# The eleven expert blocks computed during the one-hot stage: from one fp32 matmul on the raw weights to three matmuls on a rounded part and a rest, both made on GpSimd

## The chip, the cores and the metric

The kernel runs on one core of a Trainium2 chip. The metric is the device time of one execution in microseconds (us), the median of the runs shown. The engines are named as in the profile: PE is TensorE (with PEld, its weight loads), DVE is VectorE, ACT is ScalarE, POOL is GpSimd, SP is the engine that issues the DMAs here.

## The reference, cut to what matters

The program is a network of two blocks of two layers each for 256 tokens of width 1024. The second block ends each layer with a sparse feed-forward of 16384 experts (128 blocks of 128). For each token and each of 8 heads it picks 16 experts, and adds up their outputs:

```python
xt = hn.reshape(T, D_MODEL)
# idx, gate: the 16 chosen experts of each token and head, and their softmax weights
ub = u_tab[ib]
vb = v_tab[ib]
act = jax.nn.gelu(jnp.einsum('td,thkd->thk', xb, ub).astype(F32), approximate=False)
return jnp.einsum('thk,thkd->td', (gb * act).astype(vb.dtype), vb)
```

The kernel doesn't gather. It computes the activation of all 16384 experts for all tokens, multiplies it with a matrix of gates that is zero for experts not chosen, and multiplies the result with all of `peer_v`.

## The kernel before, in words

All of this is in `peer(l)`, which runs twice, once for each layer of the second block. Its parts, in the order of the program:

1. The normalised input is transposed into `xT`, a pair of tiles: `xTh`, rounded to the type fp32r, and `xTl`, the rest. An addition on DVE (L1640) puts the two together again as `xT32`, in full fp32.
2. `route` finds the chosen experts, above all on DVE. Meanwhile the activations of expert blocks 0 to 35 (`NB` = 36) are computed by `act`: a block's weights (128 x 1024, 512 KB) come by DMA into `raw`, ACT casts them into `hi` (fp32r), GpSimd subtracts to get `lo` (L290, `eng` is `nc.gpsimd`), and `mm3` issues three fp32r matmuls for each of 8 slices: hi with xTh, hi with xTl, lo with xTh.
3. **The one-hot stage** builds the gate matrix `G` (experts by tokens) four tokens at a time, in 64 steps. `one_hot` makes two tiles of comparisons on DVE, `B` (L1677) and `A` (L1679); the gates are multiplied into `A` on ACT (L1681), and for one token of every second step on DVE (L1683). Four fp32 matmuls multiply A and B into the PSUM bank `gps` (L1703). DVE multiplies the first 36 blocks of the result into `G` (L1705), and ACT copies the other 92 (L1706). `one_hot` runs three steps ahead of the matmuls.
4. In every sixth step of that stage (tokens 8, 32, 56, ... 248, eleven times) one expert block from 36 on is computed ahead. Its `raw` weights go straight into eight fp32 matmuls with `xT32` (L1696, on the trace two PE instructions each), into half a PSUM bank that is kept until the stage is over.
5. Then the rest: activations of blocks 47 to 127, and the product with `peer_v` into `pacc`.

Tiles come from pools of rotating buffers: a tile waits until the tile that had its buffer has been read for the last time. `raw`, `hi` and `lo` have three buffers each, and the tiles of `one_hot` (`oh`) are taken from the same buffers, in turns under the tags `hi` and `lo`. `gps` has two PSUM banks. A scheduler sets the order in which instructions stand on each engine when the program is built; on the chip each engine works through its queue in that order.

Of the kernel before, what the change touches and what calls it, by code (L numbers as in the profile page):

```python
# [10 lines left out]
F32 = mybir.dt.float32  # L11
# [5 lines left out]
OP = mybir.AluOpType  # L17
# [3 lines left out]
S, D, P = 256, 1024, 128  # L21
# [176 lines left out]
class Net:  # L198
# [90 lines left out]
        self.nc.scalar.copy(out=hi, in_=src)  # L289
        (eng or self.nc.vector).tensor_tensor(out=lo, in0=src, in1=hi.bitcast(F32), op=OP.subtract)  # L290

    def chunk(self, ap, n, raw_only=False, eng=None):

        raw = self.wp.tile([P, 1024], F32, tag="raw", name="raw", bufs=3)
        self.nc.sync.dma_start(out=raw[:, :n], in_=ap)
        if raw_only:
            return raw[:, :n]
        hi = self.wp.tile([P, 1024], F32R, tag="hi", name="hi")
        lo = self.wp.tile([P, 1024], F32R, tag="lo", name="lo")
        self.split(raw[:, :n], hi[:, :n], lo[:, :n], eng)  # L300
        return hi[:, :n], lo[:, :n]

    def mm3(self, ps, lh, ll, rh, rl, start, stop):
# [1318 lines left out]
    def peer(self, l):  # L1622
        nc, a, c = self.nc, self.a, self.c
        with ExitStack() as st:
            xp = st.enter_context(self.tc.tile_pool(name=f"pp{l}", bufs=1))
            xT = self.norm_t(xp, f"norm_ffn_2_{l}", "xT", 3)
# [9 lines left out]
            i2T = xp.tile([P, S], F32, name="i2T")  # L1636
            gT = xp.tile([P, S], F32, name="gT")
            keep = [[xp.tile([P, P], F32, name=f"{n}{t}") for n in ("ix1", "ix2", "gt")] for t in range(2)]
            xT32 = st.enter_context(self.tc.tile_pool(name=f"px{l}", bufs=1)).tile([P, 8, S], F32, name="xT32")
            nc.vector.tensor_tensor(out=xT32, in0=xT[0].bitcast(F32), in1=xT[1].bitcast(F32), op=OP.add)  # L1640
            NB = self.NB

            def carve(lo, n):
# [7 lines left out]
            self.lin_b(xT, a[f"pwq_{l}"], lambda b, ps: nc.scalar.copy(out=qT[:, b], in_=ps))  # L1651
            turns = [self.route(l, t, qT, sub, carve, base + 24, keep[t], i1T, i2T, gT) for t in range(2)]

            def act(b, ps, eng=None):
                hi, lo = self.chunk(a[f"pu_{l}"][b].rearrange("p k n -> p (k n)"), 1024, eng=eng)
                for k in range(8):
                    sl = slice(k * P, k * P + P)
                    self.mm3(ps, hi[:, sl], lo[:, sl], xT[0][:, k], xT[1][:, k], k == 0, k == 7)
                return ps

            for b in range(NB):
                if b == 24:
                    turns[0]()
                nc.scalar.activation(out=G[:, b], in_=act(b, self.bank("ps")[:, :S], nc.gpsimd), func=AF.Gelu)
# [4 lines left out]
            ahead = []  # L1669
            def one_hot(t0):  # L1670

                oh = self.wp.tile([P, 1024], F32, tag=("hi", "lo")[t0 // TB % 2], name="oh")
                oh = oh.rearrange("p (s t a) -> p s t a", s=2, t=TB)
                A, B = oh[:, 0], oh[:, 1]
                io = lambda n: c["iota"][:, None, :].to_broadcast([P, n, P])
                tb = lambda x, n: x[:, t0:t0 + n, None].to_broadcast([P, n, P])
                nc.vector.tensor_tensor(out=B, in0=io(TB), in1=tb(i2T, TB), op=OP.is_equal)  # L1677
                na = TB - (t0 // TB) % 2
                nc.vector.tensor_tensor(out=A[:, 0:na], in0=io(na), in1=tb(i1T, na), op=OP.is_equal)  # L1679
                for t in range(na):  # L1680
                    nc.scalar.activation(out=A[:, t], in_=A[:, t], func=AF.Copy, scale=gT[:, t0 + t:t0 + t + 1])  # L1681
                for t in range(na, TB):
                    nc.vector.tensor_scalar(A[:, t], c["iota"], i1T[:, t0 + t:t0 + t + 1], gT[:, t0 + t:t0 + t + 1],  # L1683
                                            op0=OP.is_equal, op1=OP.mult)
                return A, B

            ready = [one_hot(t0) for t0 in range(0, 3 * TB, TB)]
            for t0 in range(0, S, TB):
                if t0 % 24 == 8 and len(ahead) < 11:
                    i = len(ahead) % 2  # L1690
                    if i == 0:
                        pa = self.bank("ps" if len(ahead) < 8 else "pox")
                    pi = pa[:, i * S:i * S + S]
                    w = self.chunk(a[f"pu_{l}"][NB + len(ahead)].rearrange("p k n -> p (k n)"), 1024, raw_only=True)
                    for k in range(8):
                        nc.tensor.matmul(pi, lhsT=w[:, k * P:k * P + P], rhs=xT32[:, k], start=k == 0, stop=k == 7)  # L1696
                    ahead.append(pi)
                if t0 + 3 * TB < S:
                    ready.append(one_hot(t0 + 3 * TB))
                A, B = ready.pop(0)  # L1700
                ps = self.bank("gps")
                for t in range(TB):
                    nc.tensor.matmul(ps[:, t * P:t * P + P], lhsT=A[:, t], rhs=B[:, t], start=True, stop=True)  # L1703
                pv = ps.rearrange("p (t b) -> p b t", t=TB)
                nc.vector.tensor_tensor(out=G[:, 0:NB, t0:t0 + TB], in0=G[:, 0:NB, t0:t0 + TB], in1=pv[:, 0:NB], op=OP.mult)  # L1705
                nc.scalar.copy(out=G[:, NB:, t0:t0 + TB], in_=pv[:, NB:])  # L1706
# [6 lines left out]
            for j, ps in enumerate(ahead):  # L1713
                gated(NB + j, ps)
            NA = NB + len(ahead)
            gated(NA, act(NA, self.bank("aps")[:, :S]))
            acc = [[self.bank("pacc") for _ in range(2)] for _ in range(2)]
            last = []
            for b in range(NE):
                if NA <= b < NE - 1:  # L1720
                    gated(b + 1, act(b + 1, self.bank("aps")[:, :S]))
                wh = wk.tile([P, S], F32R, name="pwh")
                wl = wk.tile([P, S], F32R, name="pwl")
                self.split(G[:, b], wh, wl)
                hi, lo = self.chunk(a[f"pv_{l}"][b], 1024)
                last.append((b, wh, wl, hi, lo))

                if b < NE - 2 or b == NE - 1:
                    for t in range(2):
                        for b_, wh, wl, hi, lo in last:  # L1730
                            for n in range(2):
                                self.mm3(acc[t][n], wh[:, t * P:t * P + P], wl[:, t * P:t * P + P],
                                         hi[:, n * 512:n * 512 + 512], lo[:, n * 512:n * 512 + 512], b_ == 0, b_ == NE - 1)
                    last = []
            hr = []
            for t in range(2):
                raw = self.wp.tile([P, 1024], F32, tag="raw", name="raw", bufs=3)
# [8 lines left out]
    NB = 36  # L1746
# [102 lines left out]
```

## Time and profile before

| what | us |
|---|---|
| median of 3 runs | 3409.68 (3405.24 to 3410.45) |
| the profiled execution | 3410.51 |
| its span in the trace | 3408.7 |
| PE busy | 3280.5 (96% of the span) |
| DVE busy | 2251.4 (66%) |
| ACT busy | 1761.8 (52%) |
| POOL busy | 240.4 (7%) |

The span goes from the first to the last instruction in the trace, and 1.8 us of the execution lie outside it. A busy share is a mean over stages with different limits, and says little of one stage. "Idle before" is time for which an engine stood still ahead of an instruction, and the arrow names what ended it. A row of the windows view has the stretch, its length, the busy time and the number of instructions of PE, PEld, DVE, ACT and POOL, PE's granted clock as a share of full speed, the DMA engines' share and their GB/s. A row of a timeline has start, duration, engine, line, operation, out<-in and shapes.

### The profile page before, as it was taken

The page shows a single profiled execution, that of the slowest core. Times are in us where ns is not written, and L with a number is a line of the kernel's source. Part 1 is how long each engine was busy: PE and PEld are TensorE (multiplying, and loading weights), DVE is VectorE, ACT ScalarE, POOL GpSimd, SP SyncE. Part 2 cuts the span into 40 slices and gives each one's busy share as a digit, 9 for nine tenths or more (in the row PEclk, how much of TensorE's full clock was granted, in tenths as well). Part 3 has the DMA queues.
Part 4 walks back from the last instruction along what each step waited for, and adds up shares of the span by engine and source line. Part 5 has one row for each costly group of instructions (what it writes and reads, how often), then busy time and mean ns, then how long its engine had stood idle before and what let it go on. Part 6 is the DMA issues. An engine that isn't in the chain of part 4 may idle for free.

```text
span 3408.7 us, 53956 instructions
## 1 busy us (share of the span) xinstructions
PE 3280.5 (96%) x20870; PEld 2894.5 (85%) x20870; DVE 2251.4 (66%) x3881; ACT 1761.8 (52%) x3226; POOL 240.4 (7%) x159
## 2 busy tenths in 40 slices
PE   8999999999998999988999999999999899999999
PEld 7678998677997988888988999988888898899998
DVE  6676556666557776589965555567658996555555
ACT  4555445554445554435944444456444495444444
POOL 0000000000000000064000000000005500000000
PEclk9999999999999999999999999999999999999999
DMA  5435665444555345543255555555544315555555
GB/s 187 145 124 188 221 207 187 138 144 155 186 188 173 128 149 179 182 142 112 82 191 187 188 189 186 187 192 172 186 157 144 127 63 192 187 189 187 186 188 177
DMA packets 161105, 570.00 MB, mean 167 GB/s; under 512 B 18256, under 2 KB 23760, under 8 KB 159824
## 3 DMA queue, kind: packets, MB, share of 16 engines
q1 hardware_dynamic: 160848, 566.56, 50.1%
q8 instruction: 163, 2.67, 0.3%
q14 instruction: 94, 0.77, 0.1%
HBM read 557.05 MB, written 9.44 MB: 166 GB/s over the span
## 4 chain that ended last, share of the span: by engine, by line
PE 62%; DVE 10%; ACT 2%; DMA 1%; issue 1%; POOL 0%; DVEq 0%; POOLq 0%; ACTq 0%; SPq 0%
PE pacc L305 7%; PE pacc L307 7%; PE pacc L306 7%; PE aps L305 5%; PE aps L306 5%; PE aps L307 4%; PE ps L307 3%; PE ps L305 3%; PE ps L306 3%; PE gps L1703 3%; PE ps L1696 2%; PE fps L305 1%; PE fps L306 1%; PE fps L307 1%; DVE G L1789 1%; DVE G L1813 1%
## 5 line engine op out<-in xcount | busy, mean ns | idle before, releaser
L290 DVE TENSOR_TENSOR lo<-raw,hi 128x1024 fp32r<-128x1024 f32 (+3 forms) x906 | 1102.8, 1218 | 795.1 <-ACT hi L289 789.8
L289 ACT CAST hi<-raw 128x1024 fp32r<-128x1024 f32 (+1 forms) x978 | 1020.1, 1044 | 932.4 <-issue 199.6
L305 PE MATMUL pacc<-hi,pwh 128*128 128x512 f32 x1024 | 404.3, 395 | 0.1
L307 PE MATMUL pacc<-hi,pwl 128*128 128x512 f32 x1024 | 403.6, 394 | 0.0
L306 PE MATMUL pacc<-lo,pwh 128*128 128x512 f32 x1024 | 402.8, 393 | 0.0
L305 PE MATMUL aps<-xTh,hi 128*128 128x256 f32 x1296 | 365.1, 282 | 0.9 <-ACT G L1706 0.9
L306 PE MATMUL aps<-xTl,hi 128*128 128x256 f32 x1296 | 365.0, 282 | 0.0
L307 PE MATMUL aps<-xTh,lo 128*128 128x256 f32 x1296 | 363.7, 281 | 0.0
L305 PE MATMUL ps<-xTh,hi 128*128 128x256 f32 x960 | 276.9, 289 | 21.5 <-ACT hi L289 17.6
L307 PE MATMUL ps<-xTh,lo 128*128 128x256 f32 x960 | 276.2, 288 | 15.0 <-POOL lo L290 15.0
L289 ACT CAST pwh<-G 128x256 fp32r<-128x256 f32 x256 | 103.8, 406 | 342.2 <-DVE G L1711 213.9
L306 PE MATMUL ps<-xTl,hi 128*128 128x256 f32 x960 | 275.0, 287 | 1.2 <-DVE xTl L290 1.2
L305 PEld LDWEIGHTS aps<-xTh,hi 128*128 128x128 f32 x1296 | 243.8, 188 | 7.8 <-ACT G L1706 1.3
L306 PEld LDWEIGHTS aps<-xTl,hi 128*128 128x128 f32 x1296 | 243.7, 188 | 7.2
L307 PEld LDWEIGHTS aps<-xTh,lo 128*128 128x128 f32 x1296 | 243.7, 188 | 0.0
L307 PEld LDWEIGHTS pacc<-hi,pwl 128*128 128x128 f32 x1024 | 192.5, 188 | 45.5 <-DVE pwl L290 0.3
L305 PEld LDWEIGHTS pacc<-hi,pwh 128*128 128x128 f32 x1024 | 192.7, 188 | 38.7 <-ACT pwh L289 1.0
L306 PEld LDWEIGHTS pacc<-lo,pwh 128*128 128x128 f32 x1024 | 193.2, 189 | 37.5
L305 PEld LDWEIGHTS ps<-xTh,hi 128*128 128x128 f32 x960 | 185.5, 193 | 23.2 <-ACT hi L289 18.5
L290 POOL TENSOR_TENSOR lo<-raw,hi 128x1024 fp32r<-128x1024 f32 x72 | 192.0, 2677 | 179.8 <-ACT hi L289 179.8
L305 PE MATMUL fps<-fTh,hi 128*128 128x256 f32 x704 | 199.8, 284 | 4.5 <-ACT fTh L289 4.5
L307 PEld LDWEIGHTS ps<-xTh,lo 128*128 128x128 f32 x960 | 185.5, 193 | 16.5 <-POOL lo L290 16.5
(652 smaller groups left out, 6961.8 us busy)
## 6 DMA issues: line engine op xcount, KB each, us to landing
raw<-in_pu_dram SPq DMA_DIRECT2D x256, 512.0 KB, 3.3
raw<-in_pv_dram SPq DMA_DIRECT2D x256, 512.0 KB, 3.3
raw<-in_wbg_dram SPq DMA_DIRECT2D x48, 512.0 KB, 3.6
raw<-in_ffg_dram SPq DMA_DIRECT2D x44, 512.0 KB, 3.3
raw<-in_ffu_dram SPq DMA_DIRECT2D x44, 512.0 KB, 3.3
raw<-in_ffd_dram SPq DMA_DIRECT2D x44, 512.0 KB, 3.3
raw<-in_win_dram SPq DMA_DIRECT2D x36, 512.0 KB, 3.3
raw<-in_pwq_dram SPq DMA_DIRECT2D x32, 512.0 KB, 3.3
```

The costliest lines, as they stand in the source:

```text
L289: self.nc.scalar.copy(out=hi, in_=src)
L290: (eng or self.nc.vector).tensor_tensor(out=lo, in0=src, in1=hi.bitcast(F32), op=OP.subtract)
L305: mm(ps, lhsT=lh, rhs=rh, start=start, stop=False)
L306: mm(ps, lhsT=lh, rhs=rl, start=False, stop=False)
L307: mm(ps, lhsT=ll, rhs=rh, start=False, stop=stop)
L1696: nc.tensor.matmul(pi, lhsT=w[:, k * P:k * P + P], rhs=xT32[:, k], start=k == 0, stop=k == 7)
L1703: nc.tensor.matmul(ps[:, t * P:t * P + P], lhsT=A[:, t], rhs=B[:, t], start=True, stop=True)
L1789: nc.vector.tensor_tensor(out=cv[:, h], in0=vv[:, h, 0, :, None].to_broadcast([P, 16, 16]), in1=vv[:, h, 1, None, :].to_broadcast([P, 16, ...
L1813: nc.vector.tensor_tensor(out=eq, in0=eq, in1=iv[:, :, s, None, :].to_broadcast([P, 8, 16, 16]), op=OP.mult)
```

## The change

The eleven blocks computed ahead are treated as the others: `act` computes them, with three fp32r matmuls for each slice. Cast and subtraction both go to GpSimd, since `chunk` gets a second engine, `cast`. `xT32` and its addition go.

```diff
-    def chunk(self, ap, n, raw_only=False, eng=None):
+    def chunk(self, ap, n, raw_only=False, eng=None, cast=None):
...
-        self.split(raw[:, :n], hi[:, :n], lo[:, :n], eng)
+        if cast is None:
+            self.split(raw[:, :n], hi[:, :n], lo[:, :n], eng)
+        else:
+            cast.tensor_copy(hi[:, :n], raw[:, :n])
+            eng.tensor_tensor(out=lo[:, :n], in0=raw[:, :n], in1=hi[:, :n].bitcast(F32), op=OP.subtract)
...
-            xT32 = st.enter_context(self.tc.tile_pool(name=f"px{l}", bufs=1)).tile([P, 8, S], F32, name="xT32")
-            nc.vector.tensor_tensor(out=xT32, in0=xT[0].bitcast(F32), in1=xT[1].bitcast(F32), op=OP.add)
...
-            def act(b, ps, eng=None):
-                hi, lo = self.chunk(a[f"pu_{l}"][b].rearrange("p k n -> p (k n)"), 1024, eng=eng)
+            def act(b, ps, eng=None, cast=None):
+                hi, lo = self.chunk(a[f"pu_{l}"][b].rearrange("p k n -> p (k n)"), 1024, eng=eng, cast=cast)
...
-                    w = self.chunk(a[f"pu_{l}"][NB + len(ahead)].rearrange("p k n -> p (k n)"), 1024, raw_only=True)
-                    for k in range(8):
-                        nc.tensor.matmul(pi, lhsT=w[:, k * P:k * P + P], rhs=xT32[:, k], start=k == 0, stop=k == 7)
-                    ahead.append(pi)
+                    ahead.append(act(NB + len(ahead), pi, nc.gpsimd, nc.gpsimd))
```

The change also moves instructions. On GpSimd, at the end of the route of the second block's first layer, the subtractions for blocks 0 to 35 were followed by the next stage's work (`r` is a reciprocal root of a later norm). Before:

```order
L290 TENSOR_TENSOR lo_15766<-raw_15763,hi_15765 128x1024
L290 TENSOR_TENSOR lo_15798<-raw_15795,hi_15797 128x1024
L290 TENSOR_TENSOR lo_15830<-raw_15827,hi_15829 128x1024
L431 TENSOR_TENSOR r_22527<-v_22525,mhalf_163 128x1
L431 TENSOR_TENSOR r_22534<-v_22532,mhalf_163 128x1
```

and in the changed kernel (the line numbers are its own):

```order
L290 TENSOR_TENSOR lo_15793<-raw_15790,hi_15792 128x1024
L290 TENSOR_TENSOR lo_15825<-raw_15822,hi_15824 128x1024
L303 CAST hi_15914<-raw_15912 128x1024
L304 TENSOR_TENSOR lo_15915<-raw_15912,hi_15914 128x1024
L303 CAST hi_16028<-raw_16026 128x1024
L304 TENSOR_TENSOR lo_16029<-raw_16026,hi_16028 128x1024
```

Eleven pairs of a cast (L303) and a subtraction (L304) stand there now, for each layer.

On PE, around the fifth block computed ahead (the one of token 104), the rows of before are these; a `gps` row is the four matmuls of one step, here from token 96 on, a `ps` row is a matmul of the block:

```order
L1703 MATMUL gps_16217<-oh_16158 128x128 x4
L1703 MATMUL gps_16231<-oh_16172 128x128 x4
L1696 MATMUL ps_16294<-xT32_13854,raw_16295 128x256 x2
L1703 MATMUL gps_16245<-oh_16186 128x128 x4
L1703 MATMUL gps_16259<-oh_16210 128x128 x4
L1696 MATMUL ps_16294<-xT32_13854,raw_16295 128x256
L1703 MATMUL gps_16273<-oh_16224 128x128 x4
```

and these stand in the changed kernel at the same block:

```order
L1702 MATMUL gps_16362<-oh_16313 128x128 x4
L309 MATMUL ps_16369<-xTh_13709,hi_16372 128x256
L310 MATMUL ps_16369<-xTl_13710,hi_16372 128x256
L1702 MATMUL gps_16407<-oh_16327 128x128 x4
L311 MATMUL ps_16369<-xTh_13709,lo_16373 128x256
L309 MATMUL ps_16369<-xTh_13709,hi_16372 128x256
...
L311 MATMUL ps_16369<-xTh_13709,lo_16373 128x256
L1702 MATMUL gps_16421<-oh_16341 128x128 x4
L1702 MATMUL gps_16435<-oh_16355 128x128 x4
```

The block's matmuls were spread over six steps; now two stand behind the step of token 100 (`gps_16362`) and 22 in one piece behind that of token 104 (`gps_16407`), ahead of the steps of tokens 108 and 112.

On DVE, from the multiplication of step 104 into `G` on, the changed kernel has these rows (L1679 makes B, L1681 makes A, L1685 one token's gates, L1704 multiplies a step's result into `G`; `oh_16414` is of token 120, `oh_16442` of token 128, `oh_16428` of token 124):

```order
L1704 TENSOR_TENSOR G_13841<-G_13841,gps_16407 128x36x4
L1679 TENSOR_TENSOR oh_16414<-cst_142,i2T_13843 128x512
L1681 TENSOR_TENSOR oh_16414<-cst_142,i1T_13842 128x512
L1679 TENSOR_TENSOR oh_16442<-cst_142,i2T_13843 128x512
L1679 TENSOR_TENSOR oh_16428<-cst_142,i2T_13843 128x512
L1704 TENSOR_TENSOR G_13841<-G_13841,gps_16421 128x36x4
```

The comparison for token 128 stands in the queue ahead of the multiplication of step 108 (`gps_16421`). By the rotation of the `hi` buffers (tokens 96, 104, 112, then the block's `hi`, then 120, 128) it takes the buffer of token 112's tile, `oh_16355`, which `gps_16435` reads.

## Rows read from the trace of the kernel before

**Rows 1.** Windows, first one-hot stage: busy us by engine, PE's granted clock, DMA.

```profile
1592.44:1689.70 97.26, 95.67 (x684) 88.99 (x684) 95.11 (x221) 90.63 (x286) 0.00 (x0) 1.00 0.18 61
```

**Rows 2.** Chain in order of time, inside the first one-hot stage: start, length, what.

```profile
1604.67 0.43 PE ps L1696 x2
...
1612.01 1.78 PE gps L1703 x16
```

**Rows 3.** DVE's timeline in the first one-hot stage: start, duration, instruction.

```profile
1642.10 0.30 DVE L1705 TENSOR_TENSOR G<-G,gps 128x144 f32<-128x144 f32 x1
1642.32 0.69 DVE L1677 TENSOR_TENSOR oh<-cst,i2T 128x512 f32<-128x512 f32 x1
1642.92 0.56 DVE L1679 TENSOR_TENSOR oh<-cst,i1T 128x384 f32<-128x384 f32 x1
1643.39 0.30 DVE L1705 TENSOR_TENSOR G<-G,gps 128x144 f32<-128x144 f32 x1
1643.60 0.35 DVE L1683 TENSOR_SCALAR oh<-cst,i1T,gT 128x128 f32<-128x128 f32 x1
1643.86 0.69 DVE L1677 TENSOR_TENSOR oh<-cst,i2T 128x512 f32<-128x512 f32 x1
```

**Rows 4.** PE's timeline, matmuls in three parts.

```profile
1413.60 0.28 PE L306 MATMUL ps<-xTl,hi 128*128 128x256 f32 x1
1413.72 0.28 PE L307 MATMUL ps<-xTh,lo 128*128 128x256 f32 x1
```

**Rows 5.** DVE's timeline, the addition for `xT32` and the instruction behind it.

```profile
1414.37 2.29 DVE L1640 TENSOR_TENSOR xT<-xTh,xTl 128x2048 f32<-128x2048 f32 x1
1417.52 1.23 DVE L290 TENSOR_TENSOR lo<-raw,hi 128x1024 fp32r<-128x1024 f32 x1 [0.87 <-ACT hi L289]
```

**Rows 6.** POOL's timeline, three subtractions at the end of the first route.

```profile
1581.69 3.52 POOL L290 TENSOR_TENSOR lo<-raw,hi 128x1024 fp32r<-128x1024 f32 x1 [1.41 <-ACT hi L289]
1585.17 4.44 POOL L290 TENSOR_TENSOR lo<-raw,hi 128x1024 fp32r<-128x1024 f32 x1
1589.57 2.39 POOL L290 TENSOR_TENSOR lo<-raw,hi 128x1024 fp32r<-128x1024 f32 x1
```

**Rows 7.** DVE's timeline around the same time.

```profile
1568.17 0.22 DVE L1808 TENSOR_SCALAR G<-G 128x128 uint32<-128x128 uint32 x1
...
1577.97 2.39 DVE L1808 TENSOR_SCALAR G<-G 128x128 uint32<-128x128 uint32 x1
...
1580.66 2.29 DVE L1811 TENSOR_TENSOR G<-G,cst 128x2048 f32<-128x2048 f32 x1
1582.99 4.37 DVE L1813 TENSOR_TENSOR G<-G 128x2048 f32<-128x2048 f32 x1
1587.39 2.29 DVE L1814 TENSOR_REDUCE ix<-G 128x128 f32<-128x2048 f32 x1
1589.67 2.85 DVE L1677 TENSOR_TENSOR oh<-cst,i2T 128x512 f32<-128x512 f32 x1
```

**Rows 8.** A group of POOL by line, then one timeline row each of POOL and DVE.

```profile
L1552 POOL MEMSET hq<- 128x2048 f32 x1 | 1.8, 1812 | 67.3 <-DVE hqe L1538 67.3
...
71.53 1.22 POOL L672 COPY kcr<-rot 128x128 f32<-128x128 f32 x1 [39.70 <-DVE rot L523]
...
71.38 1.22 DVE L290 TENSOR_TENSOR lo<-raw,hi 128x1024 fp32r<-128x1024 f32 x1
```

**Rows 9.** ACT's timeline: the gates of four tokens, then a copy into G.

```profile
1607.01 1.28 ACT L1681 ACTIVATE oh<-oh,gT 128x128 f32<-128x128 f32 x4
1608.19 0.45 ACT L1706 COPY G<-gps 128x368 f32<-128x368 f32 x1
```

**Rows 10.** Windows in the first route, columns as in Rows 1.

```profile
1505.00:1510.00 5.00, 0.79 (x2) 0.50 (x2) 5.00 (x5) 4.31 (x7) 2.78 (x1) 0.65 0.00 0
1510.00:1515.00 5.00, 3.52 (x16) 3.52 (x17) 5.00 (x3) 0.00 (x0) 5.00 (x3) 0.50 0.41 117
...
1525.00:1530.00 5.00, 3.06 (x24) 2.64 (x23) 5.00 (x30) 1.33 (x2) 5.00 (x3) 1.00 0.53 161
```

## The prediction, made before the changed kernel ran

> **What bounds the kernel now.** The change touches two stretches, the one-hot stages of the two layers, so I read them before anything else. First the windows over the first stage, from DVE's second one-hot instruction to its last [rows 1]: in 97.3 us PE is busy for 95.7, DVE for 95.1, ACT for 90.6 and POOL for nothing, at full clock. The second stage reads alike. So three engines are full at once, and one is empty.
>
> Then the chain that ended last, in order of time. Within the stage it consists of PE alone: 16 instructions of L1703 (two steps) in 1.78 us, and two of L1696 in 0.43 [rows 2]. By this PE's work in a stage is 64 steps of 0.89 us, which is 57.0, and 11 blocks of 16 x 0.215 = 3.44 us, which is 37.8: 94.8 us.
>
> Then DVE's timeline. Start to start, L1677 takes 0.60 us, L1679 on three tokens 0.47, L1683 0.26 and L1705 0.22 [rows 3]; L1679 on four tokens has L1677's size, so 0.60. Two steps need 2 x (0.60 + 0.22) + 0.60 + 0.47 + 0.26 = 2.97 us, and 32 pairs 95.0 us. That is what the window shows as busy, so DVE has 2.2 us to spare in a whole stage. The chain names PE, but DVE is as full.
>
> **What the change removes.** A block costs PE 24 matmuls at 0.12 us start to start [rows 4], 2.88 us in place of 3.44. That is 0.56 us a block, 12.3 us for 22 blocks. It counts only where DVE delivers sooner, and DVE has 2.2 us to give in a stage.
>
> The addition for `xT32` takes 2.29 us of DVE, twice. Behind it DVE stands idle for 0.87 us until ACT's next cast is there [rows 5], so the next subtraction can't start sooner without it. I cost it at nothing; without that cover it would be 4.6 us gained in all.
>
> The DMAs of `raw` are the same in number and size.
>
> **What it adds: 44 instructions on GpSimd.** In each stage there are eleven casts and eleven subtractions of 128 x 1024. POOL is empty, so their own time is not the question, but what they do to DVE is. The end of the first route shows both at work at once. A subtraction that nothing delays takes 2.39 us (at 1589.57) [rows 6]. The one at 1581.69 takes 3.52: DVE's L1811, with two inputs in SBUF, was running until 1582.95. Then the subtraction ran, and L1813, issued at 1582.99, took 4.37 us, where L1811 of the same shape took 2.29. The next subtraction took 4.44, since it had to wait for L1813. L1808 took 2.39 where it takes 0.22 alone. And L1677, the very instruction of the one-hot stage, took 2.85 us at 1589.67, just behind a subtraction issued at 1589.57, where it takes 0.69. L1814, which has one input, ran at its usual 2.29 beside a subtraction [rows 3, 6, 7]. So a subtraction on POOL and such an instruction on DVE exclude each other. DVE loses 2.17 (L1808), 2.08 (L1813) and 2.16 us (L1677): I take 2.17. And at 1582.95 POOL, which had waited longer, went ahead of L1813, so POOL waits for one DVE instruction at most and is not starved.
>
> The Trainium skill, in "SBUF — State Buffer", section "Who interferes with whom", speaks against the change: a DVE instruction with two SBUF inputs and a GpSimd instruction that reads SBUF use one read interface, and whichever is second stands still for the whole of the other. By that rule DVE would lose all of 2.39 us; the trace agrees on the mechanism and gives 0.2 us less, which is 4.8 us over 22 subtractions.
>
> The cast has no row. From below: a MEMSET on POOL, without an input, takes 1.81 us for 2048 columns, so 0.91 for 1024. From above: the subtraction's 2.39. A copy of 128 columns took 1.22 us, but DVE's L290 (two inputs) ran from 71.38 to 72.60, and the copy ended at 72.75: about 0.2 us of its own, and a copy is shut out in the same way [rows 8]. At the MEMSET's rate 128 columns are 0.11 us, at the subtraction's 0.30; 0.2 us with a start-up in it is nearer to the first, so I take 1.0 us, of which DVE loses 0.8 by the same difference of 0.2.
>
> The Trainium skill's "GPSIMD Engine Reference", section "4.1 Engine selection", has one-input operations run at about line rate; at the 1.2 GHz that the page gives, this makes an estimate of 0.85 us for 1024 columns, and the sum would be 3 us lower. No row here shows a cast on GpSimd.
>
> **Price of a block on DVE: 2.17 + 0.8 = 3.0 us** (2.9 to 4.3 with the bounds of the cast). DVE has no spare time and works in order, so behind each held comparison stand the next ones and L1705, and behind those ACT and PE.
>
> **What the new order adds.** The rows of the change show the block of token 104 on PE: two matmuls that need `hi`, the step of token 104, then 22 in one piece, the first of which needs `lo`. Count from the start of the cast. It ends at 1.0; one comparison of DVE gets through (0.6); the subtraction then holds DVE for 2.2, until 3.8. DVE then ends step 108's comparisons (0.47), and ACT, in its order, scales three tokens (four take 1.18 us to the start of the copy behind them, so 0.9) and only then copies step 96 out of its PSUM bank (0.45) [rows 9]. At 5.6 step 104 has a bank. It ends at 6.5, the 22 matmuls at 9.1, steps 108 and 112 at 10.9. DVE, free from 3.8 on, needs 0.47 + 0.26 + 0.22 + 1.20 + 0.22 + 1.33 + 0.22 + 1.20 = 5.1 us for what stands ahead, and reaches the comparison of token 128 at 8.9. That one takes the buffer which step 112 reads, so it waits until 10.9: 2.0 us. Every second block has its step split around the 22 matmuls; there the comparison in question stands 1.4 us earlier in DVE's queue, at 7.5, and its buffer is free at 9.1, a wait of 1.6. Mean: 1.8 us. The last block of a stage has no comparison behind it. Bounds: 0, if DVE's time in hand covers PE's, and 2.6, all 22 matmuls.
>
> **The sum.** A layer: 11 x 3.0 + 10 x 1.8 - 2.2 (DVE's present idle time, contained in the new waits) = 48.8 us; both: 97.6. The profiled execution took 3410.5 us, its span 3408.7 and 1.8 around it. That gives 3508; the median before is 0.8 below the profiled execution, so **3507 us**, 2.9% slower.
>
> **Rivals.**
> *Only the holds count* (DVE's and PE's waits overlap entirely): 22 x 3.0 - 4.4 = 61.6, so 3471 us. For it: PE has 8.2 us of work in some 13. Against it: PE's order is fixed, and puts the block in one piece ahead of steps that DVE's buffers wait for. Chance 0.14.
>
> *The cast costs as much as the subtraction*: 22 x 1.37 = 30 us more, 3537. It lies within my case, whose chance is 0.70 and whose own range is 3480 to 3545.
>
> *PE's clock falls.* After PE had been busy for 0.79 us in 5, the granted clock was 0.65 and then 0.50 of full, 1.2 GHz; with 1.9 us idle in 5 it stayed at 1.00 [rows 10]. The gap before step 104, from the end of the block's first two matmuls, soon after 1.0, to 5.6, less the work of one step, is of some 3 to 4 us in 13. If the block's period on PE (six steps of 0.89 and 2.88, 8.2 us) ran at half clock throughout, it would take 16.4 us in place of the 13.7 that DVE needs (8.9 + 3.0 + 1.8): 22 x 2.7 = 59 more, 3566. Chance 0.08.
>
> *The other side: POOL does not hold DVE in this stage*, or by less than 0.2 us a block (4.4 us over 22), from which point the change is not slower. Then DVE's 95.0 us a stage set the end, PE's 12.3 us go into slack, and at most DVE's idle 2 x 2.2 us come back: 3405, which is within 0.2%. For it: all held rows are from the route, at its end. Against it: L1677 at 1589.67 is the stage's own instruction. Chance 0.05; with the addition's 4.6 us it could just pass 0.2%. The rest, 0.03, is for what I don't see.
>
> **Numbers.** 0.2%, 6.8 us, is about what a measurement of this kernel can tell from no change. Faster by more: 0.03, same: 0.04, slower: 0.93. The range goes from below the holds alone with a cheap cast (22 x 2.9 - 4.4 = 59, so 3469) to the half-clocked PE at 3566: 3458 to 3570, a few us beyond either.
>
> **What the profile would show.** Right: L304 on POOL at about 2.4 us or more and L303 near 1.0; some comparisons (L1679, L1681) of 1.5 to 2.9 us in place of 0.69, 20 or more to a stage; a stage of some 146 us in which DVE is still the fullest and PE waits for POOL's `lo` and for ACT's copies. Wrong: comparisons all at 0.69; a stage under 105 us; a cast of several us; a PE clock under 0.9 over the stage.

## The result, and the profile after

The changed kernel takes 3482.52 us (median of 4 runs, 3476.30 to 3488.27), the kernel before 3407.46 in the same comparison: a ratio of 1.0224 [1.0211, 1.0236], 75 us slower. The prediction was 3507 us with a range from 3458 to 3570. Direction and range held; the loss is 75 us where the sum said 98.

The page of the changed kernel's profiled execution, its head and the shares of the chain:

```profile
span 3480.4 us, 54367 instructions
...
PE 3294.9 (95%) x21046; PEld 2903.6 (83%) x21046; DVE 2305.6 (66%) x3879; ACT 1767.3 (51%) x3226; POOL 320.4 (9%) x203
...
PE 19%; DVE 5%; POOL 1%; ACT 1%; issue 0%; DVEq 0%; POOLq 0%; ACTq 0%
```

DVE is busy for 54 us more than before, and POOL for 80. The shares of the chain are of the whole span and add up to 26% only, since the chain of this run reaches back no further than the second route; they say nothing of the first stage. In the second stage, from 2745 to 2885, it runs through the comparisons on DVE (22.1 and 11.6% of that stretch), the subtractions on POOL (11.6%) and the steps on PE (7.8%). Before, PE's steps and blocks made 79% of it there, so the chain was mostly PE's [rows 2], and now it holds DVE and POOL. First I look at whether the 72 us between the spans lie in the two one-hot stages. A stage goes from the first comparison for B on DVE to the first `aps` matmul on PE, behind the stage. These lines summarise one line or tile in a window, which need not hold the whole stage, so the counts differ: durations as minimum, median and maximum in ns, then the first and the last start. Before, first layer and then second:

```profile
L1677 DVE TENSOR_TENSOR oh<-cst,i2T x45: 678/687/2847, 1589.7 to 1659.0; 128x512 f32<-128x512 f32 x45
L305 PE MATMUL aps<-xTh,hi x8: 279/282/384, 1695.0 to 1697.6; 128*128 128x256 f32 x8
...
L1677 DVE TENSOR_TENSOR oh<-cst,i2T x64: 679/687/2916, 2708.2 to 2806.7; 128x512 f32<-128x512 f32 x64
L305 PE MATMUL aps<-xTh,hi x56: 279/282/384, 2813.6 to 2978.2; 128*128 128x256 f32 x56
```

and after (L1679 makes B there, L309 is the first of the three matmuls):

```profile
L1679 DVE TENSOR_TENSOR oh<-cst,i2T x35: 676/684/2918, 1585.9 to 1657.5; 128x512 f32<-128x512 f32 x35
L309 PE MATMUL aps<-xTh,hi x8: 279/282/385, 1728.5 to 1731.1; 128*128 128x256 f32 x8
...
L1679 DVE TENSOR_TENSOR oh<-cst,i2T x31: 678/684/2925, 2745.1 to 2809.6; 128x512 f32<-128x512 f32 x31
L309 PE MATMUL aps<-xTh,hi x8: 279/282/390, 2885.3 to 2887.9; 128*128 128x256 f32 x8
```

Before, the stages last 105.3 and 105.4 us; after, 142.6 and 140.2. That is 37.3 and 34.8 more, 72.1 in all, and the spans differ by 71.7 (the first stage begins 3.8 us earlier, and the stretch between the stages is 3.4 longer). So the loss lies in the stages, and what is left to ask is on what DVE spends it. DVE's groups of the stage, before:

```profile
L1677 DVE TENSOR_TENSOR oh<-cst,i2T 128x512 f32<-128x512 f32 x128 | 92.4, 722 | 0.0
L1679 DVE TENSOR_TENSOR oh<-cst,i1T 128x512 f32<-128x512 f32 (+1 forms) x128 | 79.4, 621 | 0.0
L1705 DVE TENSOR_TENSOR G<-G,gps 128x144 f32<-128x144 f32 x128 | 38.7, 302 | 6.8 <-PE gps L1703 5.6
L1683 DVE TENSOR_SCALAR oh<-cst,i1T,gT 128x128 f32<-128x128 f32 x64 | 22.0, 344 | 0.0
```

and after, with POOL's two groups behind them:

```profile
L1681 DVE TENSOR_TENSOR oh<-cst,i1T 128x512 f32<-128x512 f32 (+1 forms) x128 | 117.5, 918 | 0.0
L1679 DVE TENSOR_TENSOR oh<-cst,i2T 128x512 f32<-128x512 f32 x128 | 109.8, 864 | 8.7 <-PE ps L310 7.1 <-PE pox L310 1.6
L1704 DVE TENSOR_TENSOR G<-G,gps 128x144 f32<-128x144 f32 x128 | 38.1, 297 | 11.9 <-PE gps L1702 11.7
L1685 DVE TENSOR_SCALAR oh<-cst,i1T,gT 128x128 f32<-128x128 f32 x64 | 23.3, 364 | 0.0
...
L304 POOL TENSOR_TENSOR lo<-raw,hi 128x1024 fp32r<-128x1024 f32 x22 | 58.4, 2653 | 3.4 <-ACT G L1705 1.8
L303 POOL CAST hi<-raw 128x1024 fp32r<-128x1024 f32 x22 | 23.5, 1067 | 178.7 <-DVE oh L1681 151.2 <-PE gps L1702 27.5
```

The three kinds of comparisons (two tiles and the one-token form) were busy for 92.4 + 79.4 + 22.0 = 193.8 us and are now for 250.6, with the same work: 56.8 us in which they are held, 2.58 for each of 22 blocks. DVE's idle time in front of these groups was 6.8 us and is 20.6, so 13.8 more. Together that is 70.6 of the 72.1 us.

One block shows how, in the timeline around its cast:

```profile
1645.19 1.12 POOL L303 CAST hi<-raw 128x1024 fp32r<-128x1024 f32 x1 [8.81 <-DVE oh L1681]
...
1645.54 1.31 DVE L1679 TENSOR_TENSOR oh<-cst,i2T 128x512 f32<-128x512 f32 x1
...
1646.28 0.45 ACT L1705 COPY G<-gps 128x368 f32<-128x368 f32 x1
1646.38 2.67 POOL L304 TENSOR_TENSOR lo<-raw,hi 128x1024 fp32r<-128x1024 f32 x1
...
1646.77 2.83 DVE L1681 TENSOR_TENSOR oh<-cst,i1T 128x512 f32<-128x512 f32 x1
1646.78 1.16 PE L1702 MATMUL gps<-oh 128*128 128x128 f32 x8
...
1649.11 0.39 PE L311 MATMUL ps<-xTh,lo 128*128 128x256 f32 x1 [1.17 <-POOL lo L304]
...
1651.82 1.95 PE L1702 MATMUL gps<-oh 128*128 128x128 f32 x16
...
1652.48 1.28 DVE L1679 TENSOR_TENSOR oh<-cst,i2T 128x512 f32<-128x512 f32 x2
...
1663.92 0.69 DVE L1679 TENSOR_TENSOR oh<-cst,i2T 128x512 f32<-128x512 f32 x1 [0.83 <-PE ps L310]
```

The cast holds L1679 for 1.31 us in place of 0.69 [rows 3], the subtraction holds L1681 for 2.83: 0.62 + 2.14 = 2.76 us in this block. POOL in turn waits only for the rest of the comparison that is running, which makes 2.67 of a subtraction that takes 2.39 alone [rows 6]. The last row, which belongs to the next block, is the wait for a buffer. What ends it is L310, the last matmul that reads that block's `hi`, so the comparison takes the buffer of `hi` itself. There are 12 such waits in the two stages, one in every second block or so, all ended by L310, and they make the 8.7 us that stand in L1679's group. The rows at 1651.82 and 1652.48 come back in the account of the prediction.

Last the clock, in windows of the first stage, the second column from the end being the DMA share and the one ahead of it the granted clock:

```profile
1590.00:1605.00 15.00, 11.52 (x82) 10.88 (x80) 11.31 (x21) 10.00 (x33) 3.39 (x2) 0.89 0.16 56
...
1635.00:1650.00 15.00, 10.76 (x82) 9.76 (x82) 14.16 (x24) 9.02 (x28) 5.16 (x3) 1.00 0.11 36
```

In the seven windows from 1605 to 1710 it is 1.00, the upper of the two levels (2.4 GHz); a window at 0.89 was in part at the lower (1.2). DVE stays the fullest engine, as in the second row, and PE, which was full before [rows 1], is now busy for some three quarters.

### The profile page after: what moved, and what is told of

Read it like the earlier page. It is cut to its first block, busy times and chain, and to the rows that moved or that the text cites. A ratio compares the mean times of both kernels' runs of the same rounds, so it can differ in the third digit from the quotient of the medians.

```text
span 3480.4 us, 54367 instructions
## 1 busy us (share of the span) xinstructions
PE 3294.9 (95%) x21046; PEld 2903.6 (83%) x21046; DVE 2305.6 (66%) x3879; ACT 1767.3 (51%) x3226; POOL 320.4 (9%) x203
## 5 line engine op out<-in xcount | busy, mean ns | idle before, releaser
L309 PE MATMUL pacc<-hi,pwh 128*128 128x512 f32 x1024 | 404.1, 395 | 0.1
L310 PE MATMUL pacc<-lo,pwh 128*128 128x512 f32 x1024 | 403.3, 394 | 0.0
L309 PE MATMUL aps<-xTh,hi 128*128 128x256 f32 x1296 | 366.2, 283 | 1.3 <-ACT G L1705 1.3
L310 PE MATMUL aps<-xTl,hi 128*128 128x256 f32 x1296 | 364.4, 281 | 0.0
L311 PE MATMUL ps<-xTh,lo 128*128 128x256 f32 x1088 | 314.0, 289 | 34.6 <-POOL lo L304 19.4
L309 PE MATMUL ps<-xTh,hi 128*128 128x256 f32 x1088 | 314.3, 289 | 21.5 <-ACT hi L289 17.6
L310 PE MATMUL ps<-xTl,hi 128*128 128x256 f32 x1088 | 311.3, 286 | 1.2 <-DVE xTl L290 1.2
L289 ACT CAST pwh<-G 128x256 fp32r<-128x256 f32 x256 | 103.8, 406 | 339.3 <-DVE G L1710 213.9
L309 PEld LDWEIGHTS aps<-xTh,hi 128*128 128x128 f32 x1296 | 243.9, 188 | 8.4 <-ACT G L1705 1.7
L310 PEld LDWEIGHTS aps<-xTl,hi 128*128 128x128 f32 x1296 | 244.3, 188 | 7.4
L311 PEld LDWEIGHTS ps<-xTh,lo 128*128 128x128 f32 x1088 | 209.5, 193 | 39.3 <-POOL lo L304 22.5
L309 PEld LDWEIGHTS ps<-xTh,hi 128*128 128x128 f32 x1088 | 209.8, 193 | 23.3 <-ACT hi L289 18.4
L309 PEld LDWEIGHTS pacc<-hi,pwh 128*128 128x128 f32 x1024 | 192.8, 188 | 38.6 <-ACT pwh L289 1.0
L310 PEld LDWEIGHTS pacc<-lo,pwh 128*128 128x128 f32 x1024 | 193.3, 189 | 37.9
L310 PEld LDWEIGHTS ps<-xTl,hi 128*128 128x128 f32 x1088 | 209.8, 193 | 1.7 <-DVE xTl L290 1.6
```

Source lines behind the costliest of these rows:

```text
L309: mm(ps, lhsT=lh, rhs=rh, start=start, stop=False)
L310: mm(ps, lhsT=lh, rhs=rl, start=False, stop=False)
L311: mm(ps, lhsT=ll, rhs=rh, start=False, stop=stop)
```

## The experiments

Each kernel was timed against the kernel before on the same chip, and profiled. The table has, beside the ratio, three differences to the profile of before, over both stages: the stages' length (as above; before 210.7), the busy time of the comparisons (193.8), and DVE's idle time in front of them and of the multiplication into `G` (6.8).

| version | median us | ratio | stages | comparisons | idle |
|---|---|---|---|---|---|
| changed kernel | 3482.5 | 1.0224 [1.0211, 1.0236] | +72.1 | +56.8 | +13.8 |
| e7_peonly | 3411.2 | 1.0009 [1.0000, 1.0018] | +0.6 | -1.1 | +0.1 |
| e2_memset | 3412.5 | 1.0017 [1.0008, 1.0026] | +1.5 | +11.7 | +0.9 |
| e1_hold | 3491.8 | 1.0250 [1.0236, 1.0264] | +82.5 | +57.7 | +24.0 |
| e5_own | 3473.4 | 1.0195 [1.0178, 1.0212] | +64.0 | +59.3 | +3.1 |
| e10_dose | 3535.8 | 1.0377 [1.0360, 1.0394] | +127.5 | +103.8 | +21.5 |
| e3_actcast | 3510.0 | 1.0300 [1.0280, 1.0320] | +98.4 | +42.8 | +51.8 |
| e8_actcast_own | 3459.4 | 1.0152 [1.0135, 1.0169] | +46.0 | +36.9 | +4.2 |
| e4_dvesub | 3456.6 | 1.0152 [1.0132, 1.0172] | +47.5 | -2.2 | +9.5 |
| e9_dvesub_own | 3442.5 | 1.0108 [1.0091, 1.0125] | +28.5 | -1.7 | +3.4 |

All medians lie 1 to 7 us above what the stages explain, also where the stages are as before. In the profiles the stretch from the first `aps` matmul of one stage to the start of the next is 1013.2 us before and 1015.8 to 1018.7 in e7, e2, e8 and e9. The cause of this stays open; it is about the size of what a measurement can tell.

**PE's saving alone.** Three matmuls for each slice, without POOL, `hi` or `lo`: the weights are parts of `xT`, so this kernel leaves out the activations of the 22 blocks. The addition for `xT32` is gone too. Against the kernel before:

```diff
-            nc.vector.tensor_tensor(out=xT32, in0=xT[0].bitcast(F32), in1=xT[1].bitcast(F32), op=OP.add)
...
-                        nc.tensor.matmul(pi, lhsT=w[:, k * P:k * P + P], rhs=xT32[:, k], start=k == 0, stop=k == 7)
+                        self.mm3(pi, xT[0][:, k, 0:P], xT[1][:, k, 0:P], xT[0][:, k], xT[1][:, k], k == 0, k == 7)
```

> The kernel before without xT32 and with the three fp32r matmuls per slice on the rounded input as weights: PE's saving alone, no GpSimd work in the stage, no hi or lo (the blocks' activations are not the reference's). If DVE is as full as PE: the gain is DVE's idle time at most, 0 to 4.4 us, so 3403 to 3408. If PE alone set the end: the whole 12.3 us, 3395.

Measured: 3411.2, no gain, and the stages are as long as before. So 0.56 us less PE a block is worth nothing while DVE is full, and the removed addition is worth nothing either.

**POOL's reads, with PE not waiting for them.** The changed kernel with the same weights as above in the 22 blocks (their activations are left out again): POOL casts and subtracts as in the change, but no matmul needs the result.

```diff
-                    ahead.append(act(NB + len(ahead), pi, nc.gpsimd, nc.gpsimd))
+                    self.chunk(a[f"pu_{l}"][NB + len(ahead)].rearrange("p k n -> p (k n)"), 1024, eng=nc.gpsimd, cast=nc.gpsimd)
+                    for k in range(8):
+                        self.mm3(pi, xT[0][:, k, 0:P], xT[1][:, k, 0:P], xT[0][:, k], xT[1][:, k], k == 0, k == 7)
+                    ahead.append(pi)
```

> The changed kernel with its casts and subtractions on GpSimd and its buffers, but the 264 matmuls of the blocks computed ahead take the rounded input xTh, xTl as weights in place of hi and lo, so nothing on PE waits for GpSimd (those blocks' activations are not the reference's). If DVE's being held by GpSimd is the cause: a cast lengthens a comparison by 0.62 us and a subtraction by 2.14, as in the changed kernel, so 22 x 2.76 = 61 us over the kernel before, less up to 4.4 of idle time: 3464 to 3470. If the cause is PE's in-order wait for lo: the loss is gone, 3403 to 3412.

Measured: 3491.8. The theory that PE's wait for `lo` makes the loss falls: there is no such wait, and the loss is larger. The held time is that of the change, 57.7 us. But the hold theory's number was missed by more than 20 us, and the profile says where:

```profile
L1679 DVE TENSOR_TENSOR oh<-cst,i2T 128x512 f32<-128x512 f32 x128 | 121.3, 948 | 0.1
...
L1707 DVE TENSOR_TENSOR G<-G,gps 128x144 f32<-128x144 f32 x128 | 37.9, 297 | 30.7 <-PE gps L1705 28.5 <-ACT oh L1683 2.0
```

DVE stands idle for 30.7 us before it can multiply into `G`, nearly all of it for PE's steps, where it was 6.8. PE in turn waits 58.8 us for ACT's copies to free a `gps` bank (27.2 in the changed kernel), and ACT stands behind the held comparisons. The granted clock is lower too, 0.89 in most windows of the first stage. How these 24 us divide between the two was not separated. The place of the block's matmuls is no likely reason: they stand between the steps, mostly in pieces of two to eight, and they do so too in e2, whose stages are 1.5 us longer, and in e5, where DVE's idle time grows by 3.1 us (both below).

**Writes in place of reads.** As e1, but four MEMSETs of 1024 columns stand on POOL in place of cast and subtraction, into the same `hi` and `lo` buffers (nothing reads them; the activations are left out as in e1).

```diff
-            cast.tensor_copy(hi[:, :n], raw[:, :n])
-            eng.tensor_tensor(out=lo[:, :n], in0=raw[:, :n], in1=hi[:, :n].bitcast(F32), op=OP.subtract)
+            for t in (hi, hi, lo, lo):
+                cast.memset(t[:, :n].bitcast(F32), 0.0)
```

> As the run before it, but with four MEMSETs of 128 x 1024 into the same hi and lo tiles (about 3.6 us of GpSimd a block, as long as cast and subtraction together) in place of cast and subtraction, so GpSimd writes as much and reads nothing. If what holds DVE is GpSimd's reading of SBUF: 3403 to 3412, comparisons at 0.69 us. If any work on GpSimd holds it: at least 3450. If the loss comes from the buffers that hi and lo take out of the one-hot rotation: some 3440 or more, as with cast and subtraction.

Measured: 3412.5. POOL works for 85 us in the stages (43.0 + 42.0), about as long as in the change (82), and writes into the same buffers, and the stages are only 1.5 us longer:

```profile
L1679 DVE TENSOR_TENSOR oh<-cst,i2T 128x512 f32<-128x512 f32 x128 | 89.6, 702 | 0.2
L1681 DVE TENSOR_TENSOR oh<-cst,i1T 128x512 f32<-128x512 f32 (+1 forms) x128 | 81.1, 635 | 0.0
...
L1685 DVE TENSOR_SCALAR oh<-cst,i1T,gT 128x128 f32<-128x128 f32 x64 | 34.8, 544 | 0.0
```

The comparisons with two inputs are not held at all. So it isn't POOL's being busy: the time goes where POOL reads. (What the shared buffers cost is not settled by this, since no matmul reads `hi` or `lo` here; the next version is about them.) The one-token form is held, 0.54 us against 0.34, but the next instruction on DVE starts meanwhile, so that most of it does not show in the stage. The Trainium skill, in "SBUF — State Buffer", section "Who interferes with whom", says just this of instructions with two SBUF inputs: they contend with a GpSimd instruction that reads, and not with one that only writes.

**A buffer of their own.** The changed kernel, but `hi` and `lo` of the 22 blocks come from a pool `px` of one buffer each, in the room of `xT32`, and no longer from the rotation of the one-hot tiles.

```diff
-        hi = self.wp.tile([P, 1024], F32R, tag="hi", name="hi")
-        lo = self.wp.tile([P, 1024], F32R, tag="lo", name="lo")
+        own = self.wp if cast is None else self.px
+        nb = {} if cast is None else {"bufs": 1}
+        hi = own.tile([P, 1024], F32R, tag="hi", name="hi", **nb)
+        lo = own.tile([P, 1024], F32R, tag="lo", name="lo", **nb)
```

> The changed kernel with one pair of hi and lo tiles of their own for the blocks computed ahead (in the space that xT32 left), so that they take no buffer from the one-hot tiles. If the holds are nearly all of it: only the wait of 0.83 us for the buffer in every second block goes, some 9 us, 3470 to 3478. If the shared buffers are the cause: most of the loss goes, 3410 to 3430.

Measured: 3473.4, 9 us under the changed kernel. The holds stay (59.3 us), and of the 13.8 us of added idle time 3.1 are left. So the shared buffers cost some 10 us, and the holds are nearly all of the rest. These 10 us include a change of order: with the buffers apart the scheduler spreads the block's matmuls over the steps, and the two effects were not told apart.

**Twice the dose.** e5, with the subtraction issued twice:

```diff
             eng.tensor_tensor(out=lo[:, :n], in0=raw[:, :n], in1=hi[:, :n].bitcast(F32), op=OP.subtract)
+            eng.tensor_tensor(out=lo[:, :n], in0=raw[:, :n], in1=hi[:, :n].bitcast(F32), op=OP.subtract)
```

> Own buffers, cast and subtraction on POOL, and the subtraction issued twice with the same operands (the result is the same). Hold theory (the time goes where POOL reads beside DVE's comparisons, 2.1 to 2.2 us for each subtraction): 22 x 2.15 = 47 us over 3473, so 3510 to 3530. Once-a-block theory (the loss is made once a block, by lo's coming late for PE or by the new order, and POOL's second subtraction finds DVE idle): 3473 to 3490.

Measured: 3535.8, 62 us above e5, where the hold theory said 47. The comparisons are busy for 44.5 us more than in e5, 2.02 for each added subtraction: that is the hold. DVE's idle time rises by 18.4 us, in front of the multiplication into `G`, because PE is now late with its steps:

```profile
L306 POOL TENSOR_TENSOR lo<-raw,hi 128x1024 fp32r<-128x1024 f32 x22 | 58.7, 2667 | 1.8
L307 POOL TENSOR_TENSOR lo<-raw,hi 128x1024 fp32r<-128x1024 f32 x22 | 56.0, 2546 | 1.6
...
L1708 DVE TENSOR_TENSOR G<-G,gps 128x144 f32<-128x144 f32 x128 | 38.0, 297 | 28.3 <-PE gps L1706 26.9
...
L314 PE MATMUL ps<-xTh,lo 128*128 128x256 f32 x1088 | 323.5, 297 | 69.4 <-POOL lo L307 47.4 <-POOL lo L290 22.0
```

In this group PE waits for 47.4 us for the second subtraction; in e5 it waited in the same group for 20.6 for `lo`. PE's order is fixed, so the steps behind the block wait with it. The clock was lower as well, 0.77 or 0.89 in all windows of the first stage, and how much of the 18 us is due to it stays open.

**The cast on ACT.** The changed kernel with the cast given back to ACT and the subtraction left on POOL, so that POOL reads 22 times less. First in the shared buffers:

```diff
-                    ahead.append(act(NB + len(ahead), pi, nc.gpsimd, nc.gpsimd))
+                    ahead.append(act(NB + len(ahead), pi, nc.gpsimd))
```

> The changed kernel with the cast of the blocks computed ahead on ACT, as in the other blocks, and only the subtraction on GpSimd. If the holds set the time: the cast's 0.62 us a block goes, 22 x 0.62 = 14 us, and ACT, which waits 37 us in a stage, takes 1.0 us a block unseen: 3465 to 3472; the comparisons held by the subtraction stay at 2.8 us. If GpSimd's own length on the way to lo set it (PE waits 15 us a stage for lo), the same 14 to 23 us would go, so this run tells the size of the cast's share and not the two apart.

Measured: 3510.0, 28 us slower than the changed kernel where it was to be some 14 faster. The holds did fall, to 42.8 us. DVE's idle time rose by 51.8:

```profile
L1679 DVE TENSOR_TENSOR oh<-cst,i2T 128x512 f32<-128x512 f32 x128 | 94.9, 753 | 46.5 <-PE ps L310 38.0 <-PE pox L310 8.5
...
1641.57 2.37 DVE L1685 TENSOR_SCALAR oh<-cst,i1T,gT 128x128 f32<-128x128 f32 x1
1648.25 1.29 DVE L1679 TENSOR_TENSOR oh<-cst,i2T 128x512 f32<-128x512 f32 x2 [2.89 <-PE ps L310]
```

L1679 waits for L310, the block's matmuls that read `hi`, 2.9 us in such a block. This is the kind of wait that the prediction had put at 1.8 us into the changed kernel, here at more than its upper bound. Whether it is the buffer or ACT's order was told apart by giving these 22 blocks the own buffers of e5:

> Cast on ACT, subtraction on POOL, and hi and lo of the blocks computed ahead in a buffer of their own. Buffer theory (the 2.9 us that L1679 waits for PE in each block, with the cast on ACT, is the wait for a buffer that the one-hot tiles share with hi): the wait goes, and only the holds are left, 22 x 2.0 = 45 us over 3405, so 3440 to 3465, below the version with the cast on POOL and its own buffers (3473). Order theory (ACT's cast stands behind its scalings, so the block is late on PE whatever the buffers): 3490 to 3512, as with the shared buffers.

Measured: 3459.4. The wait is gone (0.9 us left in the group, idle +4.2), the holds are 36.9 us, and the time is 51 us under e3. So it was the buffer: a comparison that has no buffer in common with `hi` can't wait for L310. The 51 us hold a change of order as well, since in e3 a block's 24 matmuls stand in one piece and here mostly in two or more. What is held now is one instruction in a block, here the one-token form:

```profile
1652.29 2.69 POOL L290 TENSOR_TENSOR lo<-raw,hi 128x1024 fp32r<-128x1024 f32 x1 [11.19 <-ACT hi L289]
...
1652.69 2.37 DVE L1688 TENSOR_SCALAR oh<-cst,i1T,gT 128x128 f32<-128x128 f32 x1
```

**The split without POOL.** Cast on ACT and subtraction on DVE, `act(NB + len(ahead), pi)`, first with shared buffers:

> The changed kernel with the cast on ACT and the subtraction on DVE itself, nothing on GpSimd in the stage. If the holds set the time: DVE pays 1.14 us a block in place of 2.76, ACT 0.95: DVE's stage goes from 95 to 95 + 11 x 1.14 = 107.5 us, so 2 x (107.5 - 97.3) = 20 us over the kernel before, 3425 to 3435, although the subtraction now stands in DVE's own queue. If the loss came from splitting the weights inside the stage at all (the order of PE, buffers): 3460 or more, as with GpSimd.

Measured: 3456.6, missed by more than 20 us. The comparisons are not held (-2.2). The 22 subtractions take 27 us of DVE (1.22 each), DVE waits for ACT's cast before most of them (6.0 us in the first stage), and the idle time in front of the one-hot work grows by 9.5: I had counted the work and left out that three engines, all nearly full, now wait for each other in order. With own buffers:

> Cast on ACT, subtraction on DVE, nothing on POOL, and hi and lo in a buffer of their own. Work theory (what this version loses is DVE's work: 22 subtractions of 1.23 us and the 0.6 us that each waits for ACT's cast, 40 us in all, less what DVE has to spare): 3440 to 3457 whatever the buffers. Buffer theory (the waits of one-hot tiles for buffers make up half of its 50 us): 3425 to 3438.

Measured: 3442.5, inside the range of the work theory, near its lower bound. The stages are 28.5 us longer, and that is DVE's added work (27) and little else. But "whatever the buffers" was wrong, and the waits for ACT's cast that this theory counted are nearly gone (0.7 us in a stage): of e4's loss, 19 us in the stages were buffers and waits. The block's matmuls stand in nearly the same order in both, 24 in one piece in e4 and 22 here. No version tried beats the kernel before.

## Why the prediction was right, and where it was off

**Right: what bounds the stage.** Three full engines [rows 1], DVE's time without slack [rows 3]: PE's saving is worth nothing (e7), and whatever holds DVE lengthens the stage one for one. In eight of the nine other versions of the table the stages grow by what DVE's comparisons, its added subtractions and its idle time (for e4 with the waits for ACT's cast) grow by, to within 5 us; e2 is the exception named above, where held time overlaps with the next instruction.

**Right: the hold.** Predicted were 2.17 us for the subtraction and 0.8 for the cast, from [rows 6, 7, 8]. The block in the timeline shows 2.14 and 0.62, its cast takes 1.12 us and the median cast 1.04, where I took 1.0. The mean over 22 blocks is 2.58 in place of 3.0, which makes 56.8 in place of 66 us. That POOL waits for one instruction of DVE at most is right as well. Half wrong is the count of long comparisons: one in each block exceeds 1.5 us, not two, since the cast leaves its own at 1.3. e2 shows that the cause is POOL's reading.

**Off: the step "What the new order adds".** It was to cost 1.8 us in 10 blocks of a layer, 36 us, less the 4.4 us of idle time that DVE had, so 31.6. DVE's idle time grew by 13.8, and the buffer wait itself is 8.7 in both layers, 0.4 us a block. Two things failed in the step.

The first is which buffer is waited for. In blocks like that of token 104 the comparison for token 128 was to wait 2.0 us until PE had done step 112. No comparison waits there. The block in the timeline is that of token 104: the two comparisons at 1652.48 are those for tokens 124 and 128, and they run without a gap until 1653.76, while PE is at steps 108 and 112 (x16) until 1653.77. So, unlike what the section on the change says, the comparison for token 128 does not take the buffer that step 112 reads: the buffers are not given out strictly in turn. In every second block, where the step is split around the 22 matmuls, the wait is the one described, for the end of these matmuls, but most are of 0.83 us where 1.6 were foreseen.

The second is the start. I had the comparisons of step 108 still ahead of DVE when the subtraction began to hold it, and so ACT's scaling and copy behind the hold, a PSUM bank for step 104 at 5.6 us, and the 22 matmuls from 6.5 us on. In the block shown, ACT's copy began at 1646.28, ahead of the subtraction, step 104 (x8 is one step) began on PE at 1646.78, 1.6 us behind the start of the cast, and the 22 matmuls began with `lo` at 1649.11, 3.9 us behind it. PE waited 1.17 us for `lo`; the prediction had a gap of some 3 to 4 ahead of step 104. e5 takes the buffers out of the rotation and gains 9 us. e3 shows how near the other case was: with the cast on ACT the wait is 2.9 us, and the loss 105 us.

**The difference, added up.** The sum of the prediction was 97.6. It is 9.2 us too large in the holds and 17.8 in the waits, which leaves the 70.6 that DVE's rows show. Of the 75 us measured, 1.5 more lie in the stages and some 3 outside them, and for these no cause was found.

**The rivals.** "Only the holds count" (3471) came nearer to 3482.5 than the main case's 3507, which it was set against: the holds are four fifths of the loss. In part that is luck: it took the holds for 66 us in place of 56.8, and let the waits overlap entirely, where 13.8 us were added. "POOL does not hold DVE" is refuted. "PE's clock falls" did not happen in the changed kernel, where the granted clock is 1.00 in the middle of the stage; in e1, e3 and e10 it did fall to 0.89 and 0.77. "The cast costs as much as the subtraction" is refuted by 0.62 against 2.14.

**Costed at nothing, and worth nothing:** the addition for `xT32` [rows 5]. Without it DVE waits for ACT's cast as foreseen:

```profile
1413.77 1.23 DVE L290 TENSOR_TENSOR lo<-raw,hi 128x1024 fp32r<-128x1024 f32 x1 [3.06 <-ACT hi L289]
```

It stood idle there for 0.87 us before, and does for 3.06 now.

## What to carry to other kernels

An empty GpSimd is not free capacity beside a full VectorE: before work that reads SBUF is moved there, look in the trace for a VectorE instruction running beside such work, and multiply what it is held for by the count of instructions that move. Ask of each tile that a change adds to a rotation whose buffer it takes and who still reads that; a small pool of its own, with the order that the scheduler then made, was worth 9 us in one version here, 14 in another and 51 in a third. A hand-made chain of waits is only as good as the position of the engines at its start, so give it both bounds and take the rows of a neighbouring block where there are any.

## What the runs showed of the hardware that I had not expected

A DVE instruction with one tile as input and its scalars from two others, L1685 (0.34 us alone, the mean of its group before), is held by POOL too: for 2.37 us beside a subtraction (e3, e8), and by MEMSETs, which don't read. In e2:

```profile
1625.39 1.97 POOL L304 MEMSET lo<- 128x1024 f32 x2 [5.16 <-DVE oh L1681]
...
1626.60 0.82 DVE L1685 TENSOR_SCALAR oh<-cst,i1T,gT 128x128 f32<-128x128 f32 x1
1626.86 0.57 DVE L1707 TENSOR_TENSOR G<-G,gps 128x144 f32<-128x144 f32 x1
```

It ends at 1627.42, with the second MEMSET (1627.36), and the instruction behind it, which starts meanwhile, with it. The comparisons L1679, with two inputs, take 0.70 us on average in this version (0.72 in the kernel before). The Trainium skill's "SBUF — State Buffer", section "Who interferes with whom", counts a `tensor_scalar` among the instructions that can take the whole shared pair of ports; these rows agree with that.
